# A float32 decoder block on one core: Strassen's scheme for 1024 columns of the FFN's gate and up

## Chip, core and metric

The kernel runs on one core of one Trainium2 chip. The metric is the device time of one execution in microseconds (us). TensorE (PE in the profile) does the matrix products, its weight loads show as PEld; VectorE (DVE) and ScalarE (ACT) do the elementwise work, GpSimd (POOL) a little, and SyncE (SP) issues nearly all transfers from HBM. Each engine runs its own list of instructions in order and waits on semaphores of the others.

## What is computed

One decoder block over 256 tokens of width 1024, all in float32. Both branches (an HGRN2 recurrence and an attention, here within one block of 256 tokens) read one normalised input; the part that the change touches is the feed-forward network (FFN) behind them and the first loads of the program.

```
D_MODEL = 1024; SEQ = 256; D_FF = 2816
proj = rmsnorm(x, attn_norm_g) @ w_in                  # 1024 x 9216; "i" is columns 2048..3071
...                                                     # recurrence, attention, gates
x  = x + merged @ w_out
h2 = rmsnorm(x, ffn_norm_g)
x  = x + (silu(h2 @ w_gate) * (h2 @ w_up)) @ w_down     # 1024 x 2816, 1024 x 2816, 2816 x 1024
```

## The kernel before

**Precision.** Every large product runs in the float32r type as three matmuls: an operand is split into a high part (`whi`, the value cast to float32r) and a low part (`wlo`, the rest), and high x high, high x low and low x high are added up in PSUM. For weights the split is made in the kernel: a 1 MB load `wraw` (128 partitions x 2048 values), then on ACT a cast to `whi` (line 55), then on DVE a subtraction to `wlo` (line 56). `split` does both, `load_w` load and split. The pool `wp` holds three buffers of each of the three, so a cast can start when the matmuls of the third-last weight tile are done.

**Two shapes of product.** `tok_block` keeps a token tile as the stationary operand and streams 512 weight columns: for each of 8 row tiles (`kt`) of the weights and 2 token tiles it issues three matmuls of 512 columns. `feat_block` keeps a 128 x 128 weight tile stationary and streams the tokens: one matmul of 512 (tokens' high and low part side by side) and one of 256 (weight's low part) for each weight tile. A block of 512 weight columns has 4 column tiles (`ct`) and 8 row tiles, in two loads of four row tiles each. Its four results lie in the four banks of the PSUM pool `pw`.

**FFN.** The 2816 columns are 22 column tiles, in groups of four (the last of two). For a group: `feat_block` for gate, evicted by `fold` (ACT copy, DVE add), scaled by `R2`, silu on ACT; `feat_block` for up, evicted, multiplied, split into `hT`; then the `down` chunks of the group before, each of two column tiles: 24 matmuls of 512 columns that add into four banks `acc`, which live to the end. The last lines add the residual and store the result.

**Ahead of the FFN** stands the product with `w_out`, in two halves. Each half adds the residual `x2`, transposes it on PE (4 x 128 columns for each token tile), multiplies by the norm's gain (`xg`), and splits into `x2T`, the FFN's input. The row sums of squares give `r2`; `spread` makes `R2` of it with two small matmuls.

**Seven products for eight** are already used elsewhere: one branch gate of 1024 columns (line 635) goes by Strassen's scheme in Winograd's form, the tokens stationary: tokens, weight rows and weight columns are halved, and 7 products of 128 tokens x 512 rows x 512 columns replace 8, with sums of the token parts (`token_sums`) and of the weight quarters (`W11` and so on, 128 x 2048 subtractions on DVE) ahead of the splits.

**Opening.** The first product is columns 2048..3071 of `w_in`. Its inputs come in small loads: gains `vec` on ACT's queue, and on SP's queue for each row tile 128 KB of x transposed (`xTr`) and 512 KB of weights, the first two row tiles' weights in halves of 256 KB.

**Order.** The kernel is written with a tile framework that schedules the instructions of each engine from the program; `tc.issue_after(i)` keeps what stands in its block behind instruction `i`. Tiles named by a `tag` share memory, and the framework adds the waits.

Of the kernel before, what the change touches and what calls it, by code (L numbers as in the profile page):

```python
# [27 lines left out]
def tile_hgrn2_moba_block(ctx: ExitStack, tc: tile.TileContext, xm, xT, vecs, table, runs,  # L28
# [29 lines left out]
    halved = []  # L58

# [28 lines left out]
    def feat_block(w, c0, act, cw=512, parts=(4, 4), cut=1):  # L88
        n = cw // P
        ps = [pw() for _ in range(n)]  # L90
        k = 0
        for pn in parts:
            hi, lo = load_w(w[k * P:(k + pn) * P, c0:c0 + cw].rearrange("(k p) c -> p k c", p=P), [pn, cw], cut)
            for ct in range(n):
                cs = slice(ct * P, (ct + 1) * P)
                for i in range(pn):
                    kt = k + i
                    both = act[kt // 4][:, kt % 4, :, :].rearrange("p m t -> p (m t)")
                    low_first = kt % 2 == 1
                    if low_first:  # L100
                        nc.tensor.matmul(ps[ct][:, 0:S], lo[:, i, cs], part(act, kt, 0), start=False, stop=False)  # L101
                    nc.tensor.matmul(ps[ct], hi[:, i, cs], both, start=(kt == 0), stop=(kt == KT - 1))  # L102
                    if not low_first:
                        nc.tensor.matmul(ps[ct][:, 0:S], lo[:, i, cs], part(act, kt, 0), start=False, stop=False)  # L104
            k += pn
        return ps
# [13 lines left out]
    xTr = big.tile([P, KT, S], F32, name="xTr", tag="T1")  # L120
# [8 lines left out]
    raws = [first(F32, "wraw")]  # L129
# [25 lines left out]
    for kt in range(KT):  # L155
        i = kt % 2
        if i == 0:
            if kt > 0:
                raws.append(first(F32, "wraw"))
            whs.append(first(F32R, "whi"))  # L160
            wls.append(first(F32R, "wlo"))
        raw, wh, wl = raws[-1], whs[-1], wls[-1]
        ks = slice(kt * P, (kt + 1) * P)
        if kt > 0:
            nc.sync.dma_start(xTr[:, kt:kt + 1, :], xT[:, kt:kt + 1, :])
            for hs in ((slice(0, 512), slice(512, D)) if kt < 2 else (slice(0, D),)):
                nc.sync.dma_start(raw[:, i, hs], w_in[ks, 2048 + hs.start:2048 + hs.stop])
        if kt == 5:
            nc.sync.dma_start(xtok, xm.rearrange("(b p) c -> p b c", p=P))
        x_hi, x_lo = part(XT, kt, 0), part(XT, kt, 1)  # L170
        if kt == 0:
            nc.scalar.copy(wh[:, i, 0:512], raw[:, i, 0:512])
            nc.vector.tensor_scalar_mul(x_hi, xTr[:, kt, :], vec[:, kt:kt + 1])
        else:
            nc.scalar.mul(x_hi, xTr[:, kt, :], vec[:, kt:kt + 1])
            nc.scalar.copy(wh[:, i, 0:512], raw[:, i, 0:512])
        nc.vector.scalar_tensor_tensor(x_lo, xTr[:, kt, :], vec[:, kt:kt + 1], x_hi.bitcast(F32),
                                       op0=OP.mult, op1=OP.subtract)
        nc.scalar.copy(wh[:, i, 512:D], raw[:, i, 512:D])
        for hs in (slice(0, 512), slice(512, D)):  # L180
            low = nc.vector.tensor_sub(wl[:, i, hs], raw[:, i, hs], wh[:, i, hs].bitcast(F32))
# [449 lines left out]
    def product(bank, act, w, first):  # L631
        hi, lo = w
        for kt in range(4):
            for m, h in ((0, hi), (0, lo), (1, hi)):
                mm = nc.tensor.matmul(bank, act(kt, m), h[:, kt, :], start=(first and kt == 0 and m == 0 and h is hi),  # L635
                                      stop=(kt == 3 and m == 1), skip_group_check=True)
# [107 lines left out]
    x2T = [big.tile([P, 4, 2, S], F32R, name=f"x2T{i}", tag=("XH", "XL")[i]) for i in range(2)]  # L744
    ss2 = small.tile([P, 2, 2], F32, name="ss2")
    for half in range(2):
        ps = tok_block(w_out, half * 512, M)
        for tb in range(2):
# [5 lines left out]
            xg = big.tile([P, 4, P], F32, name="xg", tag=("T12", "T13")[tb])  # L754
            nc.vector.tensor_mul(xg, bank.rearrange("p (k t) -> p k t", k=4),
                                 vec[:, 8 + half * 4:12 + half * 4].unsqueeze(2).to_broadcast([P, 4, P]))
            split(xg, x2T[half][:, :, 0, tb * P:(tb + 1) * P], x2T[half][:, :, 1, tb * P:(tb + 1) * P])
# [10 lines left out]
    acc = [[None, None], [None, None]]  # L768

    def down(f0, nf, act, last):  # L770
        for j0 in range(0, nf, 2):
            hi, lo = load_w(w_down[(f0 + j0) * P:(f0 + j0 + 2) * P, :].rearrange("(j p) c -> p j c", p=P), [2, D])
            end = last and j0 + 2 == nf
            for tb in range(2):
                for half in range(2):
                    ts = slice(tb * P, (tb + 1) * P)
                    cs = slice(half * 512, (half + 1) * 512)
                    if end and tb == 1 and half == 1:
                        for c0, cw in ((512, 256), (768, 256)):
                            bank = pw()  # L780
                            for i in range(2):
                                j = j0 + i
                                for m, w in ((0, hi), (0, lo), (1, hi)):
                                    nc.tensor.matmul(bank[:, 0:cw], act[:, j, m, ts], w[:, i, c0:c0 + cw],
                                                     start=(i == 0 and m == 0 and w is hi), stop=(i == 1 and m == 1))
                            xs = x2[:, tb, c0:c0 + cw]
                            nc.vector.scalar_tensor_tensor(xs, bank[:, 0:cw], r2[:, tb:tb + 1], xs,
                                                           op0=OP.mult, op1=OP.add)
                            nc.sync.dma_start(out[tb * P:(tb + 1) * P, c0:c0 + cw], xs)
                        continue  # L790
                    for i in range(2):
                        j = j0 + i
                        st = f0 + j == 0
                        en = f0 + j == (NFT - 3 if tb == 1 and half == 1 else NFT - 1)
                        nc.tensor.matmul(acc[tb][half], act[:, j, 0, ts], hi[:, i, cs], start=st, stop=False)  # L795
                        nc.tensor.matmul(acc[tb][half], act[:, j, 0, ts], lo[:, i, cs], start=False, stop=False)  # L796
                        nc.tensor.matmul(acc[tb][half], act[:, j, 1, ts], hi[:, i, cs], start=False, stop=en)  # L797
                    if end:
                        xs = x2[:, tb, cs]
                        nc.vector.scalar_tensor_tensor(xs, acc[tb][half], r2[:, tb:tb + 1], xs,  # L800
                                                       op0=OP.mult, op1=OP.add)
                        nc.sync.dma_start(out[ts, cs], xs)
            if f0 + j0 + 4 == NFT:
                xs = x2[:, 1, 512:D]
                nc.vector.scalar_tensor_tensor(xs, acc[1][1], r2[:, 1:2], xs, op0=OP.mult, op1=OP.add)

    pend = None
    for f0 in range(0, NFT, 4):
        nf = min(4, NFT - f0)
        pg = feat_block(w_gate, f0 * P, x2T, cw=nf * P)  # L810
        zt = big.tile([P, 4, S], F32, name="zt", tag=("T12", "T13")[f0 // 4 % 2])
# [15 lines left out]
        if pend is not None:  # L827
            if pend[0] == 0:
                acc = [[ph("acc00"), ph("acc01")], [pa("acc10"), pa("acc11")]]
            down(*pend, False)  # L830
        pend = (f0, nf, hT)
    down(*pend, True)


# [41 lines left out]
```

## Time and profile before

| what | value |
|---|---|
| time, median of 3 runs | 494.99 us (494.56 to 495.09) |
| the profiled execution | 495.17 us |
| its span, first to last instruction | 493.4 us |
| mean granted clock of TensorE | 0.999 |
| data moved | 91.18 MB, mean 185 GB/s |

The page of the profile gives the busy time of each engine, then the span in 40 slices, the DMA queues, the chain of work that ended last, and the costliest groups of instructions: line, engine, operation, output and inputs by tile name, shape, count, then busy time, the mean length of one in ns, and the idle time before them with what ended it. Matmuls overlap one another, so that the step from one start to the next, not the length of one, is what a matmul takes in a row of them. A timeline row gives start, length, engine, line, operation and count.

### The profile page before, as it was taken

Reading aid. Unit: us, or ns where it says so; the run is one execution under the profiler, and the core shown is the slowest. Engines: PE = TensorE matmul, PEld = TensorE weight load, DVE = VectorE, ACT = ScalarE, POOL = GpSimd, SP = SyncE. Lnnn points to the kernel's source line nnn. Section 1 sums busy time; section 2 is a strip of 40 time slices with the busy share of each in tenths; the row PEclk is TensorE's granted clock in tenths of the full one; section 3 lists DMA queues with packets and bytes.
Section 4 is the critical chain, followed back from the end, with each engine's and each line's share of the span. In section 5 each row is a group of like instructions: output and inputs, shape, how many; then the busy total and the mean of one; then the engine's idle time right before and its main releaser. Section 6 shows DMA issues by size and latency. Waiting matters only on the chain.

```text
span 493.4 us, 6683 instructions
## 1 busy us (share of the span) xinstructions
PE 487.9 (99%) x2670; PEld 412.6 (84%) x2670; DVE 365.4 (74%) x416; ACT 291.8 (59%) x408; POOL 25.5 (5%) x58
## 2 busy tenths in 40 slices
PE   8999999999999999999999999999999999999997
PEld 6888888888888888988888888888888888888885
DVE  5768999797779989499987767777636746566373
ACT  5887646777748974874664445764545435444350
POOL 0922130000000000000000000000000000000000
PEclk9999999999999999999999999999999999999999
DMA  7977595724524447327338555554565546643522
GB/s 269 395 275 257 172 304 177 245 86 160 184 84 162 146 139 266 144 83 259 128 129 276 182 182 182 184 189 171 173 209 201 185 174 189 221 143 105 191 89 85
DMA packets 43439, 91.18 MB, mean 185 GB/s; under 512 B 1928, under 2 KB 5256, under 8 KB 43408
## 3 DMA queue, kind: packets, MB, share of 16 engines
q1 hardware_dynamic: 42528, 88.09, 52.6%
q0 software_dynamic: 736, 2.65, 1.7%
q8 instruction: 21, 0.34, 0.3%
q14 instruction: 10, 0.08, 0.0%
q10 hardware_dynamic: 144, 0.02, 0.0%
HBM read 89.67 MB, written 1.07 MB: 184 GB/s over the span
## 4 chain that ended last, share of the span: by engine, by line
PE 98%; DMA 1%; SPq 0%; ACT 0%; DVE 0%; issue 0%
PE pw L102 23%; PE pw L83 10%; PE pw L84 10%; PE pw L85 10%; PE pw L101 6%; PE pw L104 6%; PE pw L152 4%; PE acc L795 4%; PE acc L797 4%; PE acc L796 4%; PE b L635 4%; PE pw L674 1%; PE pw L673 1%; PE pw L672 1%; PE ph L370 1%; DMA wraw<-w_in 1%
## 5 line engine op out<-in xcount | busy, mean ns | idle before, releaser
L56 DVE TENSOR_TENSOR wlo<-wraw,whi 128x2048 fp32r<-128x2048 f32 (+1 forms) x77 | 167.5, 2179 | 84.8 <-ACT whi L55 84.4
L55 ACT CAST whi<-wraw 128x2048 fp32r<-128x2048 f32 (+1 forms) x77 | 140.0, 1823 | 94.9 <-PE pw L85 28.7
L102 PE MATMUL pw<-x2T,whi 128*128 128x512 f32 x352 | 111.6, 395 | 0.0
L83 PE MATMUL pw<-whi,XT 128*128 128x512 f32 x144 | 56.9, 395 | 0.0
L85 PE MATMUL pw<-whi,XT 128*128 128x512 f32 x144 | 56.2, 390 | 0.0
L84 PE MATMUL pw<-wlo,XT 128*128 128x512 f32 x144 | 56.1, 390 | 0.0
L102 PEld LDWEIGHTS pw<-x2T,whi 128*128 128x128 f32 x352 | 54.1, 189 | 0.3
L101 PE MATMUL pw<-x2T,wlo 128*128 128x256 f32 x176 | 49.0, 278 | 0.0
L104 PE MATMUL pw<-x2T,wlo 128*128 128x256 f32 x176 | 48.9, 278 | 0.0
L102 PE MATMUL pw<-XT,whi 128*128 128x512 f32 x128 | 40.6, 396 | 0.0
L101 PEld LDWEIGHTS pw<-x2T,wlo 128*128 128x128 f32 x176 | 33.0, 188 | 8.0
L104 PEld LDWEIGHTS pw<-x2T,wlo 128*128 128x128 f32 x176 | 33.1, 188 | 7.4
L795 PE MATMUL acc<-whi,hT 128*128 128x512 f32 x86 | 33.5, 389 | 0.0
L797 PE MATMUL acc<-whi,hT 128*128 128x512 f32 x86 | 33.5, 389 | 0.0
L796 PE MATMUL acc<-wlo,hT 128*128 128x512 f32 x86 | 33.5, 389 | 0.0
L85 PEld LDWEIGHTS pw<-whi,XT 128*128 128x128 f32 x144 | 27.0, 188 | 5.7
L83 PEld LDWEIGHTS pw<-whi,XT 128*128 128x128 f32 x144 | 27.0, 188 | 5.6
L84 PEld LDWEIGHTS pw<-wlo,XT 128*128 128x128 f32 x144 | 27.1, 188 | 5.4
L102 PEld LDWEIGHTS pw<-XT,whi 128*128 128x128 f32 x128 | 19.9, 189 | 0.3 <-DVE Q L114 0.2
L797 PEld LDWEIGHTS acc<-whi,hT 128*128 128x128 f32 x86 | 16.1, 188 | 3.4
L796 PEld LDWEIGHTS acc<-wlo,hT 128*128 128x128 f32 x86 | 16.1, 188 | 3.4
L795 PEld LDWEIGHTS acc<-whi,hT 128*128 128x128 f32 x86 | 16.1, 188 | 3.1
(299 smaller groups left out, 864.8 us busy)
## 6 DMA issues: line engine op xcount, KB each, us to landing
wraw<-w_in SPq DMA_DIRECT2D x26, 1024.0 KB, 5.2
wraw<-w_down SPq DMA_DIRECT2D x11, 1024.0 KB, 4.9
wraw<-w_gate SPq DMA_DIRECT2D x10, 1024.0 KB, 5.2
wraw<-w_up SPq DMA_DIRECT2D x10, 1024.0 KB, 5.1
wraw<-w_in SPq DMA_DIRECT2D x10, 512.0 KB, 8.1
wraw<-w_at SPq DMA_DIRECT2D x4, 1024.0 KB, 6.0
W<-w_in SPq DMA_DIRECT2D x4, 1024.0 KB, 5.4
wraw<-w_hg SPq DMA_DIRECT2D x4, 1024.0 KB, 6.6
```

The costliest lines, as they stand in the source:

```text
L55: high = nc.scalar.copy(hi, src)
L56: return high, nc.vector.tensor_sub(lo, src, hi.bitcast(F32))
L83: nc.tensor.matmul(ps[tb], part(act, kt, 0)[:, ts], wh, start=(kt == 0), stop=False)
L84: nc.tensor.matmul(ps[tb], part(act, kt, 0)[:, ts], wl, start=False, stop=False)
L85: nc.tensor.matmul(ps[tb], part(act, kt, 1)[:, ts], wh, start=False, stop=(kt == KT - 1))
L101: nc.tensor.matmul(ps[ct][:, 0:S], lo[:, i, cs], part(act, kt, 0), start=False, stop=False)
L102: nc.tensor.matmul(ps[ct], hi[:, i, cs], both, start=(kt == 0), stop=(kt == KT - 1))
L104: nc.tensor.matmul(ps[ct][:, 0:S], lo[:, i, cs], part(act, kt, 0), start=False, stop=False)
L152: nc.tensor.matmul(ps[tb], part(XT, kt, am)[:, tb * P:(tb + 1) * P], w[:, i, hs], start=(kt == 0 and am == 0 and w is wh), stop=(kt == KT ...
L795: nc.tensor.matmul(acc[tb][half], act[:, j, 0, ts], hi[:, i, cs], start=st, stop=False)
L796: nc.tensor.matmul(acc[tb][half], act[:, j, 0, ts], lo[:, i, cs], start=False, stop=False)
L797: nc.tensor.matmul(acc[tb][half], act[:, j, 1, ts], hi[:, i, cs], start=False, stop=en)
```

## The change

Of the 22 column tiles of the FFN the last 8 (1024 columns) of gate and of up are computed by the same seven-product scheme as the branch gate, from the `x2T` halves; the other 14 stay as plain blocks. `feat_block` becomes a generator, `feat_steps`, that yields after each of its two loads. The 12 steps of the first three groups (written c below) and the 7 products of the gate scheme (P) are issued in the order `ccPcPccPccPccPcPcPc`; the last group of two column tiles follows, then the 11 down chunks, among which the 7 products of the up scheme stand. The scheme's results have tokens on the partitions: gate in `sG` (silu applied), up times gate in `U`. They are brought into the layout of `hT` by 16 transposes on PE (`turn`) and split into `hq`. The gains-times-x values are kept in float32 (`x2f`) for the token sums `C2`.

```
+    def token_sums2():
+        C = big.tile([P, 4, 4, P], F32, name="C2", tag="T3")
...
+        nc.vector.tensor_add(C[:, 0], x2f[:, 0, :, P:S], x2f[:, 1, :, P:S])
+        nc.vector.tensor_sub(C[:, 1], C[:, 0], x2f[:, 0, :, 0:P])
+        nc.vector.tensor_sub(C[:, 2], x2f[:, 0, :, 0:P], x2f[:, 0, :, P:S])
+        nc.vector.tensor_sub(C[:, 3], x2f[:, 1, :, 0:P], C[:, 1])
+        for i in range(2):
+            split(C[:, 2 * i:2 * i + 2], hi[:, 2 * i:2 * i + 2], lo[:, 2 * i:2 * i + 2])
...
+    def step(f, *args):
+        with tc.issue_after(tail[0].ins):
+            return f(*args)
...
+    def scheme(w, banks, p1, at_out, q):
...
+        product(b1, tokens(0, 0, X), halves(W11), True)
+        nc.scalar.copy(p1, b1)
+        nc.vector.tensor_sub(W11, W12, W11)
+        yield
+        product(b1, tokens(0, 1, X), halves(W21), False)
+        at_out(0, 0, b1)
+        yield
+        b3 = banks()
+        product(b3, summed(0, sums2), halves(W11), True)
+        nc.vector.tensor_sub(W11, W22, W11)
+        yield
+        b2 = banks()
+        product(b2, summed(1, sums2), halves(W11), True)
+        nc.vector.tensor_add(q(0, 1), b2, p1)
+        nc.vector.tensor_sub(W12, W22, W12)
+        yield
+        product(b2, summed(2, sums2), halves(W12), False)
+        nc.vector.tensor_add(q(1, 1), b2, p1)
+        nc.vector.tensor_add(q(1, 1), q(1, 1), b3)
+        at_out(1, 1, q(1, 1))
+        nc.vector.tensor_sub(W21, W21, W11)
+        yield
+        product(b3, summed(3, sums2), halves(W22), False)
+        nc.vector.tensor_add(q(0, 1), q(0, 1), b3)
+        at_out(0, 1, q(0, 1))
+        yield
+        product(b2, tokens(1, 1, X), halves(W21), False)
+        nc.vector.tensor_add(q(1, 0), b2, p1)
+        at_out(1, 0, q(1, 0))
+        yield
...
+    with tc.issue_after(x2_split[0].ins), tc.issue_after(x2_split[1].ins):
+        sums2 = token_sums2()
+    gate = scheme(w_gate, lambda: next(ring)("g"), gq2(1, 0), silu, gq2)
+    for what in "ccPcPccPccPccPcPcPc":
+        with tc.issue_after(x2_split[0].ins), tc.issue_after(x2_split[1].ins):
+            step(next, chunks_a if what == "c" else gate)
+    rest = plain(12, 2, 3)
+    for _ in range(4):
+        step(next, rest)
```

`tail[0]` is the last matmul of the step before. Behind this stand, each as a `step`, in this order: down, P, down, P, down, P, down, P, down, turn(0,0), P, down, P, turn(1,1), P, turn(0,1), down, turn(1,0), and four times down; P is a product of the up scheme, whose sums stand behind it. `x2_split` are the two instructions (cast and subtraction) that split the last quarter of `x2T`.

The opening loads are packed: the host lays gains, x transposed and the weight columns of a row tile side by side, and one transfer brings 1280 values for each partition; the first two row tiles come in two transfers each (803 and 512 values, then 768 and 512). The gains are read where they land.

```
-    nc.scalar.dma_start(vec, vecs)
-    nc.sync.dma_start(raws[0][:, 0, 0:512], w_in[0:P, 2048:2560])
-    nc.sync.dma_start(xTr[:, 0:1, :], xT[:, 0:1, :])
-    nc.sync.dma_start(raws[0][:, 0, 512:D], w_in[0:P, 2560:3072])
...
+        cuts = (0, NX + 512 - n0, NX + D - n0) if kt < 2 else (0, NX + D - n0)
+        for c0, c1 in zip(cuts, cuts[1:]):
+            nc.sync.dma_start(t[:, c0:c1], xw[:, kt, n0 + c0:n0 + c1])
```

**Where it moves instructions.** DVE at the seam between `w_out` and the FFN. Before, from the residual sums of the second half of `w_out` on; `wlo_2660` and `wlo_2698` are the splits of the first two gate loads, which stand ahead of these rows, `wlo_2753` is that of the first up load:

```order
L56 TENSOR_TENSOR wlo_2660<-wraw_2658,whi_2659 128x2048
L56 TENSOR_TENSOR x2T0_2464<-xg_2535,x2T0_2464 128x4x128
L56 TENSOR_TENSOR x2T0_2464<-xg_2547,x2T0_2464 128x4x128
L56 TENSOR_TENSOR wlo_2698<-wraw_2696,whi_2697 128x2048
L750 TENSOR_TENSOR x2_2302<-x2_2302,pw_2553 128x512
L750 TENSOR_TENSOR x2_2302<-x2_2302,pw_2554 128x512
L755 TENSOR_TENSOR xg_2621<-ph_2616,vec_72 128x512
L755 TENSOR_TENSOR xg_2633<-ph_2628,vec_72 128x512
L56 TENSOR_TENSOR wlo_2753<-wraw_2751,whi_2752 128x2048
```

Now, from the same sums on; `wlo_2664` is the split of the first gate load:

```order
L762 TENSOR_TENSOR x2_2297<-x2_2297,pw_2547 128x512
L762 TENSOR_TENSOR x2_2297<-x2_2297,pw_2548 128x512
L767 TENSOR_TENSOR x2f_2461<-ph_2610,vec_72 128x4x128
L767 TENSOR_TENSOR x2f_2461<-ph_2621,vec_72 128x4x128
L773 TENSOR_TENSOR r2_2631<-ss2_2462 128x2
L56 TENSOR_TENSOR x2T1_2460<-x2f_2461,x2T1_2460 128x4x128
L219 TENSOR_SCALAR r2_2631<-r2_2631 128x2
L56 TENSOR_TENSOR x2T1_2460<-x2f_2461,x2T1_2460 128x4x128
L787 TENSOR_TENSOR C2_2647<-x2f_2461 128x512
L789 TENSOR_TENSOR C2_2647<-x2f_2461 128x512
L788 TENSOR_TENSOR C2_2647<-C2_2647,x2f_2461 128x512
L56 TENSOR_TENSOR wlo_2664<-wraw_2662,whi_2663 128x2048
```

The first gate split stood ahead of the residual sums and now stands behind them, behind both splits of `x2T1` and behind three token sums.

TensorE at the same seam. Before, from the last `w_out` matmul on:

```order
L85 MATMUL pw_2554<-whi_2586,M1_2301 128x512
L102 MATMUL pw_2654<-x2T0_2464,whi_2659 128x512
L753 MATMUL ph_2616<-ident_273,x2_2302 128x128 x4
L104 MATMUL pw_2654<-x2T0_2464,wlo_2660 128x256
L101 MATMUL pw_2654<-x2T0_2464,wlo_2660 128x256
L753 MATMUL ph_2628<-ident_273,x2_2302 128x128 x4
```

Now:

```order
L86 MATMUL pw_2548<-whi_2580,M1_2296 128x512
L765 MATMUL ph_2610<-ident_268,x2_2297 128x128 x4
L765 MATMUL ph_2621<-ident_268,x2_2297 128x128 x4
L102 MATMUL pw_2658<-x2T0_2459,whi_2663 128x512
L102 MATMUL pw_2659<-x2T0_2459,whi_2663 128x512
L102 MATMUL pw_2660<-x2T0_2459,whi_2663 128x512
L102 MATMUL pw_2661<-x2T0_2459,whi_2663 128x512
L105 MATMUL pw_2658<-x2T0_2459,wlo_2664 128x256
```

Behind the transposes stand four matmuls that need only the cast of the first gate load (`whi_2663`) and then one that needs its split (`wlo_2664`).

DVE near the end of the up scheme, a stretch that before has no like (down chunks alone stood there). `wlo_3792` is the split for the seventh product, `wlo_3818` and `wlo_3855` are those of the seventh and eighth down chunk; the third row from the end makes the input of `turn(0,1)`:

```order
L856 TENSOR_TENSOR U_3562<-pw_3659,p1u_3474 128x512
L56 TENSOR_TENSOR wlo_3792<-W10_3507,whi_3791 128x2048
L857 TENSOR_TENSOR U_3562<-U_3562,pw_3610 128x512
L943 TENSOR_TENSOR U_3562<-U_3562,sG_2646 128x512
L56 TENSOR_TENSOR wlo_3818<-wraw_3816,whi_3817 128x2048
L862 TENSOR_TENSOR U_3562<-U_3562,pw_3610 128x512
L56 TENSOR_TENSOR wlo_3855<-wraw_3853,whi_3854 128x2048
L943 TENSOR_TENSOR U_3562<-U_3562,sG_2646 128x512
L56 TENSOR_TENSOR hq1_3765<-turn_3784,hq1_3765 128x4x128
L866 TENSOR_TENSOR U_3562<-pw_3659,p1u_3474 128x512
```

The split of the seventh down chunk stands ahead of the sum of the sixth product (line 862), and that of the eighth between this sum and the input of the transposes (line 943).

More of the change, by code (lines that the diff above doesn't have):

```diff
@@ L58, in tile_hgrn2_moba_block @@
     halved = []
+    tail = [None]
     def load_w(src, shape, cut=1):
@@ L101, in feat_block @@
                         nc.tensor.matmul(ps[ct][:, 0:S], lo[:, i, cs], part(act, kt, 0), start=False, stop=False)
[L102 removed]
+                    wide = nc.tensor.matmul(ps[ct], hi[:, i, cs], both, start=(kt == 0), stop=(kt == KT - 1))
+                    tail[0] = wide
                     if not low_first:
[L104 removed]
+                        tail[0] = nc.tensor.matmul(ps[ct][:, 0:S], lo[:, i, cs], part(act, kt, 0),
+                                                   start=False, stop=False)
             k += pn
+            yield
+    def feat_block(w, c0, act, cw=512, parts=(4, 4), cut=1):
+        ps = [pw() for _ in range(cw // P)]
+        for _ in feat_steps(ps, w, c0, act, cw, parts, cut):
+            pass
         return ps
@@ L765, in tile_hgrn2_moba_block @@
     R2b = R2.unsqueeze(1).to_broadcast([P, 2, S])
[L768 to L805, printed above, removed]
@@ L812, in tile_hgrn2_moba_block, with plain @@
+    def step(f, *args):
+        with tc.issue_after(tail[0].ins):
+            return f(*args)
+    def plain(f0, nf, b):
+        cw = nf * P
+        pg = [pw() for _ in range(nf)]
+        steps = feat_steps(pg, w_gate, f0 * P, x2T, cw)
+        next(steps)
+        yield
+        next(steps)
+        zt = big.tile([P, 4, S], F32, name="zt", tag=("T12", "T13")[b % 2])
         for j in range(nf // 2):
@@ L817, in tile_hgrn2_moba_block @@
             nc.scalar.activation(z, z, AF.Silu)
-        pu = feat_block(w_up, f0 * P, x2T, cw=nf * P)
+        yield
+        pu = [pw() for _ in range(nf)]
+        steps = feat_steps(pu, w_up, f0 * P, x2T, cw)
+        next(steps)
+        yield
+        next(steps)
         fl = flat()
-        hT = big.tile([P, 4, 2, S], F32R, name="hT", tag=("T5", "T6")[f0 // 4 % 2])
+        hT = big.tile([P, nf, 2, S], F32R, name="hT", tag=("T7", "T2", "T3", "T12")[b])
         for j in range(nf // 2):
@@ L826, in tile_hgrn2_moba_block @@
             split(zt[:, js, :], hT[:, js, 0, :], hT[:, js, 1, :])
[L827 to L832, printed above, removed]
+        for j in range(nf):
+            hk.append((f0 + j, hT, j))
+        yield
+    def scheme(w, banks, p1, at_out, q):
+        X = x2T
+        W11 = quarter(0, 0, "T10", w, SC)
+        W21 = quarter(1, 0, "T9", w, SC)
+        W12 = quarter(0, 1, "T11", w, SC)
+        W22 = quarter(1, 1, "T8", w, SC)
+        b1 = banks()
+        product(b1, tokens(0, 0, X), halves(W11), True)
[8 more added lines that the diff above has]
+        nc.vector.tensor_sub(W11, W22, W11)
+        yield
+        b2 = banks()
+        product(b2, summed(1, sums2), halves(W11), True)
+        nc.vector.tensor_add(q(0, 1), b2, p1)
+        nc.vector.tensor_sub(W12, W22, W12)
+        yield
+        product(b2, summed(2, sums2), halves(W12), False)
[3 more added lines that the diff above has]
+        nc.vector.tensor_sub(W21, W21, W11)
+        yield
+        product(b3, summed(3, sums2), halves(W22), False)
+        nc.vector.tensor_add(q(0, 1), q(0, 1), b3)
+        at_out(0, 1, q(0, 1))
+        yield
+        product(b2, tokens(1, 1, X), halves(W21), False)
+        nc.vector.tensor_add(q(1, 0), b2, p1)
+        at_out(1, 0, q(1, 0))
+        yield
@@ new lines, in tile_hgrn2_moba_block, with uq, hidden, turn @@
+    for what in "ccPcPccPccPccPcPcPc":
+        with tc.issue_after(x2_split[0].ins), tc.issue_after(x2_split[1].ins):
+            step(next, chunks_a if what == "c" else gate)
+    assert not list(chunks_a) and not list(gate)
+    rest = plain(12, 2, 3)
+    for _ in range(4):
+        step(next, rest)
+    U = None
+    hq = [None, None]
+    def uq(i, j):
+        return U[:, i, j * 512:(j + 1) * 512]
+    def hidden(i, j, src):
+        nc.vector.tensor_mul(uq(i, j), src, gq2(i, j))
+    def turn(i, j):
+        bank = pw("turn")
+        src = uq(i, j)
+        for k in range(4):
+            tail[0] = nc.tensor.transpose(bank[:, k * P:(k + 1) * P], src[:, k * P:(k + 1) * P], ident)
+        ts = slice(i * P, (i + 1) * P)
+        split(bank.rearrange("p (k t) -> p k t", k=4), hq[j][:, :, 0, ts], hq[j][:, :, 1, ts])
@@ new lines, in tile_hgrn2_moba_block @@
+    acc = [[ph("acc00"), ph("acc01")], [pa("acc10"), pa("acc11")]]
+    p1u = big.tile([P, 512], F32, name="p1u", tag="T15")
+    up = scheme(w_up, pw, p1u, hidden, uq)
+    step(down)
+    step(next, up)
+    step(down)
+    U = big.tile([P, 2, D], F32, name="U", tag="T7")
+    step(next, up)
+    step(down)
+    step(next, up)
+    step(down)
+    hq[0] = big.tile([P, 4, 2, S], F32R, name="hq0", tag="T2")
+    step(next, up)
+    step(down)
+    step(turn, 0, 0)
+    step(next, up)
+    step(down)
@@ L835, in _bucket @@
+    hq[1] = big.tile([P, 4, 2, S], F32R, name="hq1", tag="T3")
+    step(next, up)
+    step(turn, 1, 1)
+    step(next, up)
+    assert not list(up)
+    step(turn, 0, 1)
+    step(down)
+    for j in (1, 0):
+        for k in range(4):
+            hk.append((NPL + 4 * j + k, hq[j], k))
+    step(turn, 1, 0)
+    for _ in range(4):
+        step(down)
 def _bucket(n):
```

134 lines of the change are left out of this document (95 added, 39 removed).

## The prediction, made before the changed kernel ran

> **What bounds the kernel now.** First the page: busy shares, and the chain of work that ended last.
>
> ```profile
> span 493.4 us, 6683 instructions
> PE 487.9 (99%) x2670; PEld 412.6 (84%) x2670; DVE 365.4 (74%) x416; ACT 291.8 (59%) x408; POOL 25.5 (5%) x58
> PE 98%; DMA 1%; SPq 0%; ACT 0%; DVE 0%; issue 0%
> ```
>
> TensorE is busy for 99% of the span, and the chain runs over it. Then its waits, which the profile lists by who was waited for:
>
> ```profile
> PE warm L140 <- DVE ones L135: 1.1, 1, 1.1
> PE pw L152 <- ACT whi L179: 0.6, 1, 0.6
> ```
>
> Only the opening made TensorE wait. So the time is what TensorE has to do, and a change pays by matmuls taken away, as long as ACT and DVE still deliver every split ahead of its use. Third, the busy time by stretch: the seam into the FFN, one FFN group (gate, up, two down chunks), and the end of the span.
>
> ```profile
> 305.80:318.30 12.50, 12.50 (x76) 10.85 (x75) 9.25 (x14) 9.21 (x16) 0.00 (x0) 1.00 0.56 173
> 361.30:394.50 33.20, 33.20 (x178) 28.49 (x177) 20.41 (x21) 16.11 (x18) 0.00 (x0) 1.00 0.58 190
> 489.80:493.40 3.60, 0.00 (x0) 0.00 (x0) 0.47 (x1) 0.00 (x0) 0.00 (x0) 0.84 0.42 146
> ```
>
> The columns are the stretch and its length, busy us (count) of PE, PEld, DVE, ACT and POOL, the granted clock, DMA share, GB/s. DVE is busy for 20.41 of 33.20 us in a group, 61%.
>
> **TensorE's work.** The prices stand in the chain:
>
> ```profile
> 234.72 5.44 PE b L635 x24
> 271.69 1.05 PE ph L739 x8
> 198.58 1.78 PE ph L407 x16
> ```
>
> Two products of the branch gate's scheme (24 matmuls of 512 columns) take 5.44 us, one 2.72; a down chunk has 24 matmuls of the same size, so 5.44. A group of 33.20 less two chunks leaves 22.32 for a gate and an up block, 11.16 each. Removed are 2 x 1024 columns, four blocks: 44.6 us. Added are 14 products, 14 x 2.72 = 38.1, and 16 transposes at 1.05 for eight, 2.1. Sum: **-4.4 us** on TensorE. Nothing hides this, it is on the path.
>
> **The seam.** Before, the first gate load is cast and split while `w_out` still runs, and the sums then start as follows (each row names its engine):
>
> ```profile
> 294.15 1.91 ACT L55 CAST whi<-wraw 128x2048 fp32r<-128x2048 f32 x1 [3.53 <-DVE x L750]
> 296.19 2.28 DVE L56 TENSOR_TENSOR wlo<-wraw,whi 128x2048 fp32r<-128x2048 f32 x1
> 305.35 1.37 DVE L750 TENSOR_TENSOR x<-x,pw 128x512 f32<-128x512 f32 x2 [0.52 <-PE pw L85]
> 306.78 1.37 DVE L755 TENSOR_TENSOR xg<-ph,vec 128x512 f32<-128x512 f32 x2
> 310.27 1.29 DVE L56 TENSOR_TENSOR x2T<-xg,x2T 128x512 fp32r<-128x512 f32 x2
> 305.83 0.39 PE L102 MATMUL pw<-x2T,whi 128*128 128x512 f32 x1
> 308.36 0.63 ACT L759 ACTIVATE jk<-x 128x512 f32<-128x512 f32 x1
> 308.98 0.60 ACT L55 CAST x2T<-xg 128x512 fp32r<-128x512 f32 x1
> 311.47 0.16 DVE L761 TENSOR_TENSOR r<-ss 128x2 f32<-128x2 f32 x1
> 311.66 0.17 DVE L209 TENSOR_SCALAR r<-r 128x2 f32<-128x2 f32 x1
> L608 DVE TENSOR_TENSOR C<-F 128x512 f32<-128x512 f32 x1 | 0.7, 685 | 0.0
> ```
>
> So TensorE goes on at 305.83 with a gate matmul whose operands have lain ready for 7 us. In the changed order nothing of the gate is split by then: in DVE's own list the first gate split stands behind the residual sums, the two multiplications, both `x2T1` splits and three token sums. With this trace's starts and lengths: sums from 305.35, multiplications 306.78 to 308.15, the sum of `ss2` (0.16), split 0.65, the step for `r2` (0.17), split 0.65, three token sums at 0.6 from start to start, hence 311.6; the split then takes 2.28: **313.9**. ACT is done earlier: two squares (0.62 each, accumulator read included) from 306.1, two casts of 0.6 behind the multiplications to 308.8, the gate's cast of 1.91 to 310.6. TensorE has until 313.9 its eight transposes (1.05) and the four matmuls that need only the cast (4 x 0.23 = 0.9). Of the 8.1 us from 305.83 it uses 2.0: **+6.1 us**. What is late next on DVE is the second gate load's split, at 318.5 (worked out below), just ahead of TensorE's need at 318.9.
>
> On SP's queue two quarter loads of the scheme (W22, W21) wait for the memory of `M`, free at 305.8 with the last `w_out` matmul, and the second up load stands behind them. That load's buffer is free only with the first gate split, at 313.9, and it needs 5.1 us:
>
> ```profile
> wraw<-w_up SPq DMA_DIRECT2D x10, 1024.0 KB, 5.1
> ```
>
> It is in at 319, and its cast can't start before 327 (its buffer of `whi` is held by the first product). So the loads cost nothing, unless that cover of 8 us goes.
>
> **The clock behind the seam.** TensorE would sit idle for 3.3 us (transposes done at 307.3, cast at 310.6) and, after 0.9 us of work, for another 2.3. No row before has such a gap, the longest is the 0.6 quoted. Bounds: nothing, since the granted clock is 1.00 in every stretch of work; or half speed for a while. For the second speak the last row of the stretches, where the grant falls to 0.84 in 3.60 us without matmuls, and the start of the program:
>
> ```profile
> 1.13 3.48 PE L140 MATMUL warm<-ones 128*128 128x128 f32 x16 [1.13 <-DVE ones L135]
> ```
>
> 16 pieces of float32 products of 128 columns take 3.48 us there and 1.78 at 198.58 (line 407, the same size): half speed for 3.5 us, that is 1.7 us lost. I take **+1.7**, since the gap of 3.3 us is nearly as long as the stretch of 3.6 that lowered the grant. The Trainium skill ("TensorE: Matmul & The Clock Gate", Part 1) says that the array's clock halves after an idle window of some 3.4 us and comes back after a busy one, the window running free; the fall to 0.84 agrees. Its window, as it may start anywhere, would make the loss 1.7 to 3.4 us, an estimate by that page, and the sum up to 1.7 us more.
>
> **The mixed steps: does DVE keep up?** Prices from the groups:
>
> ```profile
> L56 DVE TENSOR_TENSOR wlo<-W,whi 128x2048 fp32r<-128x2048 f32 x7 | 15.9, 2285 | 1.2 <-ACT whi L55 1.1
> L699 DVE TENSOR_TENSOR W<-W,W 128x2048 f32<-128x2048 f32 x1 | 2.3, 2285 | 0.0
> L114 DVE TENSOR_TENSOR zt<-pw,zt 128x256 f32<-128x256 f32 x22 | 8.4, 418 | 1.1 <-ACT zt L113 0.5
> L816 DVE TENSOR_TENSOR zt<-zt,R 128x512 f32<-128x512 f32 x11 | 7.6, 687 | 0.2
> L56 DVE TENSOR_TENSOR Cl<-C,Ch 128x1024 fp32r<-128x1024 f32 x2 | 2.4, 1218 | 0.0
> ```
>
> In the 12 c and 7 P TensorE needs 12 x 5.58 + 7 x 2.72 = 86.0 us. DVE has 19 splits and 4 quarter sums at 2.2 from start to start (50.6), three groups' evictions of 8 x 0.42 + 6 x 0.69 = 7.5 (22.5), 5 sums of the scheme at 0.69 (3.4), and the token sums and their splits with the `R2` steps (6.7): 83.2, or 97% where 61% stood. Adding up DVE's list step by step against TensorE's, one place is late: the first up load's split. Behind 313.9 come `r2` and the fourth token sum 0.8, a token split 1.2, `dg` 0.5, the second gate split to 318.5, `R2` and a token split to 320.1, the W11 split to 322.3, two evictions 0.75, W12-W11 to 325.2, 1.4 of evictions, and the split to 328.8. TensorE is there at 328.2 (318.9, second gate load 5.58, product 2.72, four matmuls of the cast 0.9): 0.6 us, or 0.2 if the slow clock has held it back by then. Later steps have 1 us or more in hand, because the buffers of three let DVE run two tiles ahead. **+0.2.** That DVE runs at 97% without further loss is the least sure part. Bounds: 0, and 2.6 if the 23 large operations take their lengths of 2.29 instead of 2.2 (2.1 us) and each split waits as in the branch gate's scheme (1.2 us for 7, so 3.3 for 19): DVE then has 88.6 us to TensorE's 86.0.
>
> **The down stage.** For a chunk and a product, 8.16 us of TensorE, DVE has two splits (4.4), at most one quarter sum (2.2) and about two operations of 0.69: 8.0, and again most splits come ahead. One input is late, that of `turn(0,1)`. Count from t, the end of the fifth product. The cast of the seventh down chunk waits for the buffer of the sixth (t + 5.44) and takes 1.9; its split ends at t + 9.6, the sum behind it at 10.2, the eighth chunk's split at 12.4, the multiplication at 13.1. TensorE is there at 5.44 + 2.72 + 0.53 + 2.72 = t + 11.4. **+1.7**; bounds 0 and 3.9 (one split more ahead of it). The inputs of the other three turns are done 2 us or more ahead by the same count. The tail behind the last matmul is unchanged.
>
> **The opening.** SP issues 10 transfers instead of 18, each larger, and ACT's queue none. Before:
>
> ```profile
> 3.72 0.62 ACT L172 CAST whi<-wraw 128x512 fp32r<-128x512 f32 x1 [0.98 <-DMA wraw<-w_in]
> 6.35 0.62 ACT L179 CAST whi<-wraw 128x512 fp32r<-128x512 f32 x1 [2.01 <-DMA wraw<-w_in]
> 4.67 0.70 PE L152 MATMUL pw<-whi,XT 128*128 128x512 f32 x2
> 9.45 18.89 PE pw L152 x82
> 0.00:5.00 5.00, 3.81 (x18) 3.59 (x18) 1.69 (x4) 2.10 (x3) 0.78 (x6) 1.00 0.54 142
> ```
>
> 96 matmuls at 0.23 from 4.67 would end at 26.8; they end at 28.34, so at most 1.5 us can be won. The first transfer grows from 256 to 402 KB, at 142 GB/s of the first 5 us up to 1.1 us more, while the second half of the first weights, which came only at 6.33 behind and between others, is now the second transfer. Bounds +0.7 and -1.5; I take **-0.4**, nearer to nothing, since the bytes that have to come in are the same. Past 9.45 TensorE runs without a gap either way.
>
> **Sum.** -4.4 + 6.1 + 1.7 + 0.2 + 1.7 - 0.4 = +4.9. Against the profiled execution of 495.17 (its span and 1.8 around it) that is 500.1; against the median of 494.99, 0.2 below it, **499.8 us**.
>
> **Rivals.** (1) The clock does not fall: the 1.7 go, the first up load's wait is 0.6: 498.6. For it: 1.00 in all stretches with work; against it: the row that ends at 493.40. (2) DVE becomes the bound of the mixed steps: with the 2.6 us worked out above, 502.4; it decides as soon as waits on DVE pass the 2.8 us between 83.2 and 86.0. For it speaks the sum, against it that the splits run ahead. (3) Not slower: the seam costs little. If the first gate split is done while `w_out` still runs, as at 296.19 before, TensorE goes on after 0.4 us and the clock stays: -4.4 + 0.4 + 0.6 + 1.7 - 0.4 = -2.1, 492.9. For it: three buffers are free for the gate load, and that is how it went before; against it: DVE and ACT take their lists in order, and there the split stands behind the sums. It decides where TensorE goes on before 310.4 instead of 313.9 (with rival 1's other terms the sum is then nil). This is also the case in which the change does what it is written to do.
>
> **Chances.** Forecast 0.45 (alone 498.5 to 501.3); clock stays 0.28; DVE bound 0.10; seam cheap 0.08; the rest, 0.09, is the lower end of rival 1, with the opening at -1.5 and the turn not late: 498.6 - 1.1 - 1.7 = 495.8. A change under 0.2% (1 us) can't be told from none here. Faster: 0.08, the cheap seam. Same: 0.09, the rest. Slower: 0.83. The range, 495.7 to 501.7, takes in the forecast, rival 1 and what the opening and the turn leave open; it leaves out rivals 2 and 3, 0.18.
>
> **What would show it.** Seam: idle time of TensorE of some 6 us in one stretch between the `L765` transposes and the first `L105` matmul, released by DVE's `wlo`; the granted clock under 1.00 in the us behind it. Scheme: `L645` products at 2.72, none waiting. DVE near full in the 90 us behind the seam. A wait of `L949` for DVE near the end. Opening: the end of `L168` against 28.34. The forecast is wrong if the gate's split is found ahead of the residual sums, or if the mixed steps show a row of waits for DVE.

## The result, and the profile after

The changed kernel takes **500.0 us** (median of 5 runs, 499.42 to 500.63) where the kernel before takes 494.99 beside it: a ratio of 1.0105, 95% interval 1.0094 to 1.0116. Its profiled execution took 499.42 us, of which the span is 497.7.

The page and the waits of TensorE, to be read against those of before:

```profile
span 497.7 us, 6514 instructions
PE 486.7 (98%) x2598; PEld 408.9 (82%) x2598; DVE 398.3 (80%) x426; ACT 301.8 (61%) x402; POOL 24.7 (5%) x59
PE 94%; DVE 4%; DMA 1%; ACT 1%; issue 1%
PE pw L102 <- ACT whi L55: 3.2, 1, 3.2
PE turn L949 <- DVE U L943: 1.8, 1, 1.8
PE pw L105 <- DVE wlo L56: 1.0, 2, 0.9
```

TensorE has 72 instructions fewer and is busy for 1.2 us less, yet the program is longer. Of the chain that ends last, 2% lay off TensorE before and 6% do now. Three waits are new, 6.0 us together. The first and 0.86 us of the third are one place, the seam; the other 0.17 us of the third are the first up load's split (TensorE goes on at 328.52). The timeline at the seam, engine by engine (start, length, instructions, in brackets the idle time ahead and who ended it):

```profile
304.49 0.39 PE L86 MATMUL pw<-whi,M 128*128 128x512 f32 x1
304.98 1.34 PE L765 MATMUL ph<-ident,x 128*128 128x128 f32 x8
309.55 2.08 PE L102 MATMUL pw<-x2T,whi 128*128 128x512 f32 x4 [3.23 <-ACT whi L55]
312.48 0.58 PE L105 MATMUL pw<-x2T,wlo 128*128 128x256 f32 x1 [0.86 <-DVE wlo L56]
307.60 1.89 ACT L55 CAST whi<-wraw 128x2048 fp32r<-128x2048 f32 x1
309.54 0.69 DVE L788 TENSOR_TENSOR C<-C,x2f 128x512 f32<-128x512 f32 x1
310.14 2.29 DVE L56 TENSOR_TENSOR wlo<-wraw,whi 128x2048 fp32r<-128x2048 f32 x1
```

The last `w_out` matmul starts at 304.49 (305.60 before, so all stands 1.1 us earlier), and its successor could start at 304.72. The first gate split stands behind the third token sum in DVE's list and ends at 312.4, and TensorE goes on at 312.48. Of these 7.76 us it uses 1.05 for the transposes and 0.93 for the four matmuls of the cast: the seam costs 5.8. (The two waits make only 4.1, because the list counts the slow matmuls and the ends of matmuls as busy.)

The four matmuls of the cast at 309.55 take 2.08 us; with the clock up the same four take 1.20 (e3, below). The same place in slices of 1 us, with the granted clock in the third column from the end:

```profile
308.00:309.00 1.00, 0.00 (x0) 0.97 1.04 406
309.00:310.00 1.00, 0.46 (x1) 0.50 0.29 109
315.00:316.00 1.00, 1.00 (x5) 0.61 1.03 401
```

The grant falls to 0.50 at 308.94 (0.97 is 0.94 us at full and the rest at half) and is back at 315.78. From 312.48 on TensorE has work, so 3.3 us at half speed cost 1.65.

The other rows that the prediction named: the mixed steps, DVE over its share of them, the late turn, and the chain's opening.

```profile
320.00:407.00 87.00, 86.83 (x473) 74.70 (x472) 74.29 (x75) 54.22 (x65) 0.00 (x0) 1.00 0.58 188
310.14:404.00 93.86, 81.69 (x82) 0.97 0.56 180
391.69 2.72 PE g L645 x12
465.65 0.63 PE L949 MATMUL turn<-ident,U 128*128 128x128 f32 x4 [1.82 <-DVE U L943]
466.03 0.48 PE L902 MATMUL acc<-whi,hT 128*128 128x512 f32 x1
466.35 0.40 PE L903 MATMUL acc<-wlo,hT 128*128 128x512 f32 x1
4.98 22.31 PE pw L168 x96
```

TensorE is busy for 86.83 of 87.00 us in the mixed steps: no row of waits there. The products take their 2.72. The opening's 96 matmuls end at 27.29 (28.34 before).

### The profile page after: what moved, and what is told of

It is laid out like the page before. It is cut to its first block, busy times and chain, and to the rows that moved or that the text cites. A ratio compares the mean times of both kernels' runs of the same rounds, so it can differ in the third digit from the quotient of the medians.

```text
span 497.7 us, 6514 instructions
## 1 busy us (share of the span) xinstructions
PE 486.7 (98%) x2598; PEld 408.9 (82%) x2598; DVE 398.3 (80%) x426; ACT 301.8 (61%) x402; POOL 24.7 (5%) x59
## 4 chain that ended last, share of the span: by engine, by line
PE 94%; DVE 4%; DMA 1%; ACT 1%; issue 1%
PE pw L102 16%; PE pw L84 10%; PE pw L86 9%; PE pw L85 9%; PE pw L168 4%; PE pw L105 4%; PE pw L101 4%; PE acc L904 4%; PE acc L902 4%; PE acc L903 4%; PE b L645 4%; PE g L645 3%; PE pw L645 3%; DVE wlo L56 2%; PE pw L683 1%; PE pw L685 1%
## 5 line engine op out<-in xcount | busy, mean ns | idle before, releaser
L56 DVE TENSOR_TENSOR wlo<-wraw,whi 128x2048 fp32r<-128x2048 f32 (+1 forms) x69 | 149.0, 2164 | 37.5 <-ACT whi L55 37.3
L55 ACT CAST whi<-wraw 128x2048 fp32r<-128x2048 f32 (+1 forms) x69 | 124.7, 1813 | 61.5 <-PE pw L86 20.5
L102 PE MATMUL pw<-x2T,whi 128*128 128x512 f32 x224 | 73.5, 405 | 3.2 <-ACT whi L55 3.2
L56 DVE TENSOR_TENSOR wlo<-W,whi 128x2048 fp32r<-128x2048 f32 x21 | 47.9, 2288 | 11.1 <-ACT whi L55 10.9
L55 ACT CAST whi<-W 128x2048 fp32r<-128x2048 f32 x21 | 40.2, 1914 | 26.4 <-PE acc L904 13.6
L102 PEld LDWEIGHTS pw<-x2T,whi 128*128 128x128 f32 x224 | 36.3, 194 | 4.1 <-ACT whi L55 3.5
L105 PE MATMUL pw<-x2T,wlo 128*128 128x256 f32 x112 | 31.8, 284 | 1.0 <-DVE wlo L56 1.0
L101 PE MATMUL pw<-x2T,wlo 128*128 128x256 f32 x112 | 31.6, 282 | 0.0
L105 PEld LDWEIGHTS pw<-x2T,wlo 128*128 128x128 f32 x112 | 21.5, 192 | 6.7 <-DVE wlo L56 2.2
L101 PEld LDWEIGHTS pw<-x2T,wlo 128*128 128x128 f32 x112 | 21.5, 192 | 5.0
L902 PE MATMUL acc<-whi,hT 128*128 128x512 f32 x56 | 21.9, 391 | 0.0
L904 PE MATMUL acc<-whi,hT 128*128 128x512 f32 x56 | 21.8, 390 | 0.0
L101 PE MATMUL pw<-XT,wlo 128*128 128x256 f32 x64 | 17.8, 279 | 0.0
```

The costliest lines, as they stand in the source:

```text
L55: high = nc.scalar.copy(hi, src)
L56: return high, nc.vector.tensor_sub(lo, src, hi.bitcast(F32))
L102: wide = nc.tensor.matmul(ps[ct], hi[:, i, cs], both, start=(kt == 0), stop=(kt == KT - 1))
L105: tail[0] = nc.tensor.matmul(ps[ct][:, 0:S], lo[:, i, cs], part(act, kt, 0), start=False, stop=False)
L904: tail[0] = nc.tensor.matmul(acc[tb][half], act[:, j, 1, ts], hi[:, i, cs], start=False, stop=en)
```

## The experiments

Each was timed beside the kernel before (494.85 to 495.14 us in these comparisons).

**The first gate block freed (e1).** The changed kernel; only the first two steps lose their hold behind the x2 split:

```
-    for what in "ccPcPccPccPccPcPcPc":
+    for n, what in enumerate("ccPcPccPccPccPcPcPc"):
+        if n < 2:
+            step(next, chunks_a)
+            continue
         with tc.issue_after(x2_split[0].ins), tc.issue_after(x2_split[1].ins):
```

> The changed kernel, but its first gate block may be cast and split as soon as its loads are in (before the residual sums), as in the kernel before; nothing else changes. Theory A (the seam is a wait for DVE's split, and the slow clock behind it comes from that wait): TensorE goes on within 0.5 us of the last w_out matmul, the clock stays at 1.00, 5.8 + 1.7 us go: 492.5 us (492.0 to 493.0), faster than the kernel before. Rival B (the clock falls there for another reason): only the gap goes, 494.2. Rival C (DVE has no room in the mixed steps, the wait only moves to later splits): 495 or more, with waits of L105 for DVE further on.

493.56 us, ratio 0.9973 (0.9964 to 0.9983): 6.4 us less than the changed kernel, and faster than the kernel before. Its waits, and the timeline of TensorE and DVE where one of them is:

```profile
PE turn L952 <- DVE U L946: 1.9, 1, 1.9
PE pw L105 <- DVE wlo L56: 1.6, 1, 1.6
322.49 0.39 PE L105 MATMUL pw<-x2T,wlo 128*128 128x256 f32 x1 [1.61 <-DVE wlo L56]
317.09 1.21 DVE L56 TENSOR_TENSOR C2l<-C,C2h 128x1024 fp32r<-128x1024 f32 x1
320.15 2.28 DVE L56 TENSOR_TENSOR wlo<-wraw,whi 128x2048 fp32r<-128x2048 f32 x1
```

The seam's wait and the slow clock are gone (the grant is 1.00 throughout this stretch). But the first up load's split, 0.17 us late in the changed kernel, is 1.6 late now: TensorE arrives earlier, DVE still has the token sums and their splits ahead of it. So theory A holds for the seam, and rival C for one place of 1.6 us, which is why the time is 493.56, above theory A's range, and not 492.5.

**turn(0,1) one down chunk later (e4), and both edits (e6).** e4 is the changed kernel with

```
-    step(turn, 0, 1)
     step(down)
+    step(turn, 0, 1)
     for j in (1, 0):
```

> The changed kernel with turn(0,1) one down chunk later. Theory A (turn(0,1) waits 1.8 us for U, which is ready 1 us into the next chunk): the wait goes, 498.2 us. Rival B (the wait moves on: the first chunk that reads hq[1] then waits for the split of the turned block): 499.0 to 500.0, with a wait in L902 or L904.

498.78 us (ratio 1.0071, 1.0059 to 1.0083). The wait is gone from the list and nothing takes its place (the 1.1 us of the warm-up, which every run waits at the start of the program, are left out of these lists):

```profile
PE pw L102 <- ACT whi L55: 3.2, 1, 3.2
PE pw L105 <- DVE wlo L56: 1.0, 2, 0.9
308.00:309.00 1.00, 0.00 (x0) 0.58 1.04 408
318.00:319.00 1.00, 1.00 (x6) 0.80 0.77 117
```

It gains 1.2 us and not 1.8, because the clock took some back: in this execution the grant falls at 308.16 and is back only at 318.4, 2.6 us later than in the changed kernel, and the half of that, 1.3, is what its profile lacks (a span of 497.1, 0.6 less and not 1.8). Neither theory had that. The five executions bear it out: three with a mean grant of 0.988 took 498.78 to 499.07, two with 0.993 took 497.94 and 498.25, which is some 1.7 less than the three of the changed kernel with 0.992 or 0.993 (499.42, 499.98 and 500.0).

> Both edits together: first gate block freed and turn(0,1) one chunk later. If the two costs are separate they add: 492.5 - 1.8 = 490.7 us, 4.3 us less than the kernel before (4.4 of TensorE's work and 1.1 of the opening, less 0.5 to 1 of small waits). Rival (they share a cause, DVE being late all along, or the freed split moves DVE's work): 491.5 to 493.

492.06 us (ratio 0.9938, 0.9925 to 0.9951). With the clock at 1.00 in both, the turn is worth 493.56 - 492.06 = 1.5 us. The time itself lies where the rival put it, and for one of the rival's two reasons: the freed split moves DVE's work, and the wait of 1.6 us that e1 had brought is here too, the only one left. Measured against e1, which has that wait as well, the two edits add:

```profile
PE pw L105 <- DVE wlo L56: 1.6, 1, 1.6
```

**The token sums later (e9).** Both edits, and `token_sums2()` is called ahead of the sixth step in place of the first:

```
-    with tc.issue_after(x2_split[0].ins), tc.issue_after(x2_split[1].ins):
-        sums2 = token_sums2()
...
+        if n == 5:
+            sums2 = step(token_sums2)
```

> The kernel with both edits (492.06 us), and the token sums written behind the fifth step, so that most of their splits and the evictions stand behind the first up load's split in DVE's list. In the run with both edits that split was 1.6 us late. Theory A (DVE has a backlog behind the seam, and what is not needed yet can wait): the 1.6 us go, 490.5. Rival B (DVE is full there whatever the order, the wait moves to the next split): 491.3 to 492.

**490.06 us**, ratio 0.9901 (0.9886 to 0.9916), the fastest of all. The up load's wait is gone too, 0.2 us of the opening is all that is left. The last row is a stretch of the mixed steps, with the columns DVE, granted clock, DMA share, GB/s:

```profile
PE pw L168 <- ACT whi L186: 0.2, 1, 0.2
304.40:398.00 93.60, 83.73 (x90) 1.00 0.56 186
```

From the last `w_out` matmul's start to that of the last matmul the kernel before needs 183.87 us (305.60 to 489.47) and this one 179.76 (305.03 to 484.79). TensorE is busy for all of both stretches, so this is the work that the scheme saves: 4.1 us. The four rows, two of the kernel before and two of this one:

```profile
305.60 0.39 PE L85 MATMUL pw<-whi,M 128*128 128x512 f32 x1
489.47 0.28 PE L784 MATMUL pw<-whi,hT 128*128 128x256 f32 x1
305.03 0.39 PE L86 MATMUL pw<-whi,M 128*128 128x512 f32 x1
484.79 0.28 PE L891 MATMUL pw<-whi,hq 128*128 128x256 f32 x1
```

**The opening alone (e2).** The kernel before with the packed loads of the diff and nothing else.

> The kernel before with the packed opening loads alone (10 transfers on SP's queue in place of 18, no transfer on ACT's); its FFN is untouched. Theory A (the opening is worth what the changed kernel's trace shows, the end of L168 at 27.29 in place of 28.34): 1.05 us less than before, 494.0. Rival B (its end moved for other reasons, or the gain is given back where the first feature block starts): 494.6 (the 0.4 us of the prediction) to 495.1.

493.97 us, ratio 0.9981 (0.9972 to 0.9990), 0.9 us less. Its chain has

```profile
4.93 22.38 PE pw L160 x96
```

so these matmuls end at 27.31, nearly as in the changed kernel (27.29). This is theory A.

**The seam alone (e5).** The kernel before; its gate and up blocks are held behind the x2 split, as the changed kernel holds them:

```
+        with tc.issue_after(x2_split[0].ins), tc.issue_after(x2_split[1].ins):
+            pg = feat_block(w_gate, f0 * P, x2T, cw=nf * P)
...
+        with tc.issue_after(x2_split[0].ins), tc.issue_after(x2_split[1].ins):
+            pu = feat_block(w_up, f0 * P, x2T, cw=nf * P)
```

> The kernel before, with its first gate and up loads held behind the x2 splits as in the changed kernel, and nothing else: plain blocks, no scheme, no token sums, no quarter loads. Theory A (the order alone makes the seam): three token sums (1.8 us) fewer stand ahead of the split, so TensorE waits about 4.3 us, and the clock costs 1.7: 495.0 + 6.0 = 501.0 (500.0 to 501.5). Rival B (the gap is made by the token sums or the quarter loads): 495.5 to 497.

502.35 us, ratio 1.0148 (1.0134 to 1.0162): the order alone, without any scheme, costs 7.5 us. TensorE and DVE at the seam, then the clock:

```profile
305.23 0.39 PE L85 MATMUL pw<-whi,M 128*128 128x512 f32 x1
310.29 1.36 PE L102 MATMUL pw<-x2T,whi 128*128 128x512 f32 x4 [3.23 <-ACT whi L55]
312.62 0.58 PE L104 MATMUL pw<-x2T,wlo 128*128 128x256 f32 x1 [0.97 <-DVE wlo L56]
310.27 2.29 DVE L56 TENSOR_TENSOR wlo<-wraw,whi 128x2048 fp32r<-128x2048 f32 x1 [1.11 <-ACT whi L55]
311.00:312.00 1.00, 0.65 (x3) 0.60 0.00 0
318.00:319.00 1.00, 1.00 (x7) 0.99 0.97 354
```

Theory A in kind, but the time lies above its range, since both of its terms were short. The gap is 312.62 - 305.46 - 1.98 = 5.2 us, not 4.3: without the token sums DVE only waits 1.11 us for ACT's cast, which could not start before the casts of `x2T`. And the clock is low from 311.2 to 318.0, of which 5.4 us are work, 2.7 lost. That makes 7.9; its opening waits 0.4 us less than that of the kernel before (0.2 in place of 0.6), which leaves the 7.5.

**The gap filled with dummy matmuls (e3, e3b).** The changed kernel; dummies keep TensorE at work where it waits for the cast (14 of them, e3), and also where it waits for the split (8 more, e3b). No operand of the FFN comes earlier.

```
+    fill = pa("fill")
+    with tc.issue_after(turned.ins):
+        for _ in range(14):
+            nc.tensor.matmul(fill, ones_r, x2T[0][:, 0, :, :].rearrange("p m t -> p (m t)"), start=True, stop=True)
```

> The changed kernel with 14 dummy matmuls of 512 columns (3.25 us) between the last x2 transposes and the first gate matmul; they read tiles that are ready and write a bank that nobody reads. The gap itself stays, since DVE's split still ends at the same time. Theory A (the clock falls because TensorE sits idle for 3.2 us): the clock stays at 1.00 behind the seam, 1.7 us less (up to 2.0): 498.2. Rival B (the slow us come from something else, such as the loads that start there): 500.0, with the clock still near half.

499.56 us (ratio 1.0085, 1.0073 to 1.0097), a miss for theory A: the idle 3.2 us are gone, and in the profiled execution the clock falls all the same, only later.

```profile
306.08 3.50 PE L775 MATMUL fill<-x2T,ones_r 128*128 128x512 f32 x14
309.57 1.20 PE L102 MATMUL pw<-x2T,whi 128*128 128x512 f32 x4
312.50 0.38 PE L105 MATMUL pw<-x2T,wlo 128*128 128x256 f32 x1 [1.72 <-DVE wlo L56]
313.00:314.00 1.00, 1.00 (x6) 0.50 0.53 61
316.00:317.00 1.00, 1.00 (x8) 0.79 0.89 334
```

The four matmuls of the cast run at full speed here and end sooner, so 1.72 us of idle time are left ahead of the split. Four of the five executions have a mean grant of 0.996 or 0.997; the fifth, of the same instructions, has 1.000 and took 498.10 us. Were the 1.72 us enough to lower the clock, or is it not idle time that does it?

> As the kernel with the filled gap, with 8 more dummy matmuls (1.85 us) between the four matmuls of the cast and the first L105, so that hardly 0.2 us of the seam are idle; DVE's split still ends at the same time. In the run with one gap filled the second gap of 1.72 us was followed by 3.4 us at half speed. Theory A (idle time decides, and 1.7 us of it in the wrong place is enough): the clock stays at 1.00, 498.0 us (1.6 to 1.7 less than with one gap filled). Rival B (the slow us have nothing to do with idle time): 499.6, matmuls again at half speed from 313 to 316.

498.19 us (ratio 1.0065, 1.0052 to 1.0078). With the second gap filled as well the grant stays, in all five executions (mean 0.998 to 1.000):

```profile
PE pw L107 <- DVE wlo L56: 0.2, 1, 0.2
313.00:314.00 1.00, 1.00 (x8) 1.00 0.52 78
```

So it is idle time that lowers the clock at this seam, and a clock that stays is worth 1.8 us against the changed kernel (500.0). The dummies themselves cost nothing, they run where TensorE would wait.

**Room on DVE (e7).** On e9, dummy sums of 128x512 on DVE in each of the seven gate steps of the scheme:

```
+            for _ in range(2 if what == "P" else 0):
+                nc.vector.tensor_add(pad, x2[:, 0, 0:512], x2[:, 0, 512:D])
```

> The kernel with the sums later (490.06 us), with two dummy sums of 128x512 on DVE (0.69 us each) in each of the seven steps of the scheme's gate half, 9.6 us in all; nobody reads them. Measures the room on DVE in the mixed steps, where the prediction's rival had DVE as the bound. Theory A (DVE is busy for 83.7 of the 93.6 us of this stretch, and its splits run ahead): the load goes into the idle time, 490 to 491.5. Rival B (DVE was at 97%, as the prediction's sum had it, so that some 2.6 us of room are left): 7 us more, 497.

> The same with four dummy sums in a step, 19.3 us in all, where DVE must become the bound. Theory A (9.9 us of room): 9.4 us or a little more over 490.06: 499.5 to 501. Rival B (2.6 us of room): 16.7 us more, 506.8.

492.80 us and 499.10 us (ratios 0.9964, 0.9953 to 0.9975, and 1.0085, 1.0070 to 1.0100), that is 2.7 and 9.0 more than e9. The waits of the one and the other, and DVE in the same stretch as above (the same in us: as the run gets longer, less of the work falls into it):

```profile
PE pw L105 <- DVE wlo L56: 2.3, 2, 2.1
304.40:398.00 93.60, 89.84 (x102) 1.00 0.55 180
```

```profile
PE pw L105 <- DVE wlo L56: 6.2, 3, 3.9
304.40:398.00 93.60, 91.57 (x106) 0.96 0.50 163
```

19.3 us of load cost 9.0, so 10 us of room are there at least, near the 9.9 of theory A. Not all of the cost is waiting, though: in the profiled execution (499.74 us) 6.2 are waits, and behind the longest of them, 3.9 us, the grant falls too (0.96 in this stretch), which costs some 3 us. No run tells how much of that would have been wait instead. Nor do 9.6 us go in for free (theory A had 1.4 at most): one split is 2.1 us late. The room seems to be spread unevenly.

## Why the prediction was right

499.8 us forecast, 500.0 measured, and the mechanism is the one written down: the seam's wait, the slow clock behind it and the late turn outweigh the work saved. That the two times meet within 0.2 is luck in part: the terms as measured add up to 0.6 less than forecast, and 0.7 that stand in no term make up for it. Term by term:

- TensorE's work, -4.4: **-4.1** (e9 against before). The 16 transposes are not what lacks: in e9 they take 1.6 us (0.35, 0.35 and 0.89 for eight), not 2.1. But what stands beside them is longer: in the changed kernel the first matmul behind a turn takes 0.32 us to the next start (466.03 to 466.35), not 0.23, and in e9 the three products behind the first turn take 2.75 to 2.87, not 2.72, and the last four down chunks 0.3 more than before. Why is open.
- Seam, +6.1: **+5.8** in the trace. The list of DVE, start by start, gave it: the split's start was put at 311.6, which is 310.5 with the 1.1 us taken off by which all stands earlier, and it is 310.14. ACT's cast ends at 309.49, as worked out (310.6 less 1.1). So the token sums are only 0.65 us of the seam, and without them (e5) it is still 5.2.
- Clock, +1.7: **1.65** in the profile, 1.8 by e3b, which is rival 1 in effect: 498.2, where 498.6 was worked out. That it falls behind the gap was right, the reason given for it was too narrow: that 3.3 us is nearly as long as a stretch of 3.6 in which the grant fell. It took less: the grant fell when TensorE had been idle for 2.6 us (2.0 in e4), and in e3 1.7 us were enough. One of its two grounds is weak as well: for the start of the program, where 16 pieces ran at half speed by their pace, the row 0.00:5.00 gives a grant of 1.00. From the windows that the Trainium skill ("TensorE: Matmul & The Clock Gate", Part 1) describes, the prediction estimated a loss of 1.7 to 3.4 us. The traces agree with that spread: 1.65 here, 2.7 in e5, some 3.0 in e4.
- First up load's split, +0.2: **0.17**.
- DVE in the mixed steps, 97%: **87%** (81.69 of 93.86 us). The 81.69 hold 3.6 us of the next group's splits and leave out 1.8 of token sums, so the work to set against the forecast's 83.2 is 79.9, 4% less. The 86.0 us it was set against were too short: DVE starts on these steps one split ahead of TensorE and ends behind it, so it has 94 us. e7 shows what that means for rival 2: at least 10 us of room in all.
- turn(0,1), +1.7: **1.8**, and 1.5 by e6 against e1. DVE's list runs as it was counted: the sum of the sixth product (line 862) starts at 462.02, the eighth chunk's split at 462.61, the multiplication at 464.82, and TensorE goes on at 465.65.
- Opening, -0.4: **-0.9** (e2; 1.05 in the chain). The step that failed is the choice "nearer to nothing, since the bytes that have to come in are the same". Here it is not the bytes: the first 5 us moved 203 GB/s in place of 142. The transfer that the chain starts from ends at 4.29, where before TensorE waited for one that was in only at 6.33; the first matmul starts later than before (4.98, not 4.67), but behind it none waits. Whether the size of the transfers, their order or their number does it, no run takes apart.

```profile
0.00:5.00 5.00, 3.80 (x17) 3.51 (x17) 1.51 (x4) 2.14 (x4) 0.99 (x7) 1.00 0.64 203
0.81 3.48 DMA xw<-xw
```

The terms measured make -4.1 + 5.8 + 1.65 + 0.2 + 1.8 - 1.05 = +4.3, which is the difference of the two spans (497.7 - 493.4). The medians differ by 5.0. The other 0.7 is in part the clock: the profiled execution is the fastest of the five, and the two with the lowest mean grant, 0.990, took 500.44 and 500.63, the three with 0.992 or 0.993 took 499.42 to 500.0. The rest stays open.

Rival 3, the cheap seam, is what e1 builds: 493.56 where 492.9 was worked out. The reading was right that DVE's list decides it, and the price missed what was late next: 1.6 us of wait at the first up load, where 0.6 was put.

## What to carry to other kernels

A hold that keeps a block's loads, casts and splits behind the end of the stage ahead takes away the work-ahead that hid them: the order alone cost 7.5 us here, more than the 4.1 that the better algorithm gave. Look in the list of each preparing engine at what stands ahead of the first operand that TensorE will need, and put behind it what is not needed yet (here the token sums); with that and the moved turn the same change goes from 1% slower to 1% faster. When such a wait is removed, look for what is late next, since the consumer then arrives earlier everywhere behind it.

## What the runs showed of the hardware

The clock's slow stretches have lengths that are multiples of one length: 3.4 us in e3 (313.0 to 316.4), 6.8 in the changed kernel (308.94 to 315.78), 6.8 in e5 (311.2 to 318.0), 6.8 in the longer run of e7 (377.0 to 383.8) and 10.2 in e4 (308.16 to 318.4): one, two and three times 3.4. That fits windows of 3.4 us that run on by themselves, as the Trainium skill ("TensorE: Matmul & The Clock Gate", Part 1) describes them. By its table of states the clock halves behind an idle window; here the measurement differs, and decides: a window need not be idle to lower the grant. In e3 the 3.4 us that end at 313.0 held 1.7 us of work at full speed and one gap of 1.72 us, and were enough, though not in each execution: one of the five kept its clock with the same instructions. Nor does work end the slow time at once: in the changed kernel the four matmuls at 309.55 bring 2.08 us of work into the window behind 308.94, and the grant stays at 0.50 for another. At the turn a gap of 1.82 us left the clock alone:

```profile
466.00:467.00 1.00, 1.00 (x7) 1.00 0.91 320
```

So the length of a gap does not settle it. Where it lies against the window does not settle it either, as far as these traces go: counted on from 315.78 in steps of 3.41 us (a third of the 10.24 of e4), a window would run from about 462.6 to 466.0, hold the whole gap and 1.6 us of work, hardly less than the 1.7 that lowered the grant in e3. That is an estimate, which rests on the windows going on evenly for 147 us; what decides between the two places stays open.
